# Constants and the roots' transposition under the keys' section, and earlier loads for mixing and the second gate

## The chip, the cores and the metric

The kernel runs on one core of one Trainium2 chip. The metric is the device time of one execution in microseconds (us). The engines are named as the profile names them: PE is TensorE, DVE is VectorE, ACT is ScalarE, POOL is GpSimd, and SP is SyncE, which here only issues transfers (DMA). All loads and stores of this kernel go through SP's one queue, in order.

## What is computed

One layer of a streaming encoder: an RMS norm, one projection of all rows into queries, keys, values and gates of two groups of eight heads, stick-breaking attention (group A) and forgetting attention (group B), each output times SiLU of its gate, an output projection, and a final norm. 2048 prompt rows with 16 meta rows in front, and 32 rows of a running stream with a cache of 2048 rows. The model width is 1024, a head has 64.

```python
def project(h, g_norm, w_in, b_f):
    u = rmsnorm(h, g_norm) @ w_in
    ...
    logf = jax.nn.log_sigmoid(fl.astype(jnp.float32) + b_f.astype(jnp.float32))

def sb_block(q, k, v, q_start):
    ...
    log_keep = jnp.where(before, jax.nn.log_sigmoid(-z), 0.0)
    later = lax.cumsum(log_keep, axis=3, reverse=True) - log_keep
    w = jnp.where(before, jnp.exp(jax.nn.log_sigmoid(z) + later), 0.0)

def fox_block(q, k, v, c, q_start):
    ...
    decay = c_q[:, :, :, None] - c_k[:, :, None, :]
    p = jax.nn.softmax(jnp.where(causal, logits + decay, -jnp.inf), axis=-1)

def combine(h, oa, ga, ob, gb, w_out):
    mixed = jnp.concatenate([oa.reshape(B, T, SB_WIDTH) * jax.nn.silu(ga),
                             ob.reshape(B, T, FOX_WIDTH) * jax.nn.silu(gb)], axis=-1)
    return h + mixed @ w_out
```

## The kernel before

All matrix products of the projections are made of three products of split operands: x and w are each cast to a high part and a low remainder, and `mm3` (line 288) adds hi x hi, hi x lo and lo x hi over eight slices of the width, 24 matmuls for one group of output.

**The values' section (v1).** `SecV.run` goes over 17 row tiles t of 128 rows, two units u of 256 columns each, so 34 groups of 24 matmuls (names psv). Beside it the generator `feed` brings the rows: for a tile it loads x_T (names xraw), casts it to xh on ACT (line 1562) and subtracts on DVE to xl; it also loads the same rows untransposed in two halves (xrow), sums their squares on ACT (line 1536), and at the tiles listed in ROOTS it computes the reciprocal roots r_all on DVE and ACT (`newton`, lines 600 to 606). A group of values needs its tile's root only when ACT evacuates it: vt is the PSUM result times r_all (line 430), fl the eight columns of the forget gate (line 432). The accumulators psv share four PSUM banks (pool ps_1), so group n + 4 waits for the evacuation of group n. The evacuated vt is stored twice (out_dram, v_s).

Staging tiles come from `stage(name, type, tag)`, two tiles to a tag. vt, and in later sections kf, have the tag "kt"; xrow, rrow and the prefix sums dc have the tag "sg". In the kernel before the constants' staging tiles mf, sf and one have the tag "kt" too, and `constants()` (line 167) is called in `feed` at tile 6: it loads masks, pick matrix, rows6 and biases b_bc, casts three of them on DVE, and writes rows of ones to kb_s (five writes).

At the end of `feed` the 17 columns of roots are transposed on PE (ptr, line 1576), copied by DVE (rrow) and written to r_s in DRAM. After the values, five reads bring them back spread over all partitions (xr), because the keys' evacuation multiplies by a row of roots.

**The keys' section (k1).** 384 columns of rows at a time, two units: PE makes psTk, DVE multiplies by xr to kf (line 400), ACT casts to kx (line 401), DVE subtracts, SP stores kx twice and kf once. It uses the same four banks. Beside it `decay` runs: it finishes the forget gates fl (lines 536 to 547: abs, exp, reciprocal, log), transposes them on PE (ptf_t, line 555, and ptf, line 589), and forms prefix sums (dcp, line 567).

**Later.** The query section q1, then the forgetting attention beside further projections, then from about 1060 us the stick-breaking attention (`sb_main`), beside which `filler` runs: the first gate's last part, the second gate g1 and the output projection of group B. For each group of g1 `ahead_g` loads the attention output (og) and the reciprocal denominators (den, two reads); POOL multiplies them (line 516), DVE multiplies by the gate (line 517), SP stores to m_s. All these tiles come from one tag "k2" of six tiles. `mixing(step)` starts a mix for each finished pair of A heads and block of 512 rows: `mix_a` loads oa and gfa, DVE multiplies (line 1339), ACT takes the sigmoid in place (line 1340), DVE multiplies again (line 1342), SP stores to m_s; MW = 2 steps of the attention lie between its parts.

**What sets the order.** The framework's scheduler places the instructions on each engine's queue by its own estimate of when they are ready; the order in the program counts as their rank. On the chip each queue then runs strictly in that order, so one instruction that waits holds all behind it.

Of the kernel before, what the change touches and what calls it, by code (L numbers as in the profile page):

```python
# [7 lines left out]
F32 = mybir.dt.float32  # L8
# [9 lines left out]
NS = 32  # L18
# [42 lines left out]
HB = 0.5  # L61
MW = 2
NL = 4.0
NA = 2.0
# [24 lines left out]
def trunk_step_kernel(ctx, tc, x_all, x_T, x_K, x_V, x_Q, ca_kT, ca_v, cb_kT, cb_v, cb_lfT, norm_g, w_K, b_f,  # L89
# [77 lines left out]
    def constants():  # L167
        mf = stage("mf", F32, "kt")[:, :SEC]
        dma(mf, mask_c)
        nc.vector.tensor_copy(masks16, mf)  # L170
        sf = stage("sf", F32, "kt")
        dma(sf[:, :2 * NS], smask_c)
        dma(sf[0:8, 2 * NS:2 * NS + 128], pick_c)
        dma(rows6[64:70], rows_c)
        nc.vector.tensor_copy(ident_r, ident)
        nc.vector.tensor_copy(smasks, sf[:, :2 * NS])
        nc.vector.tensor_copy(pick, sf[0:8, 2 * NS:2 * NS + 128])
        dma(b_bc, b_f[0:1, :].broadcast_to([128, 8]))
        dma(den_s[:, NX:TQ], ones_t[0:8, :NS])
        one = stage("one", F32, "kt")[0:8, :SEC]  # L180
        nc.gpsimd.memset(one, 1.0)
        for c in range(0, T, SEC):
            n = min(SEC, T - c)
            dma(kb_s[:, 130:134, c:c + n], one[:, :n].unsqueeze(1).broadcast_to([8, 4, n]))
# [126 lines left out]
    class SecT(Units):  # L311
# [9 lines left out]
        def unit(self, u):  # L321
            return load_unit(256, KT, f"{self.nm}{u}", g_col)

        def first_x(self):
            if self.xs is None:
                self.xs = self.src(self.nm, *self.chunks[0])

        def run(self):
# [11 lines left out]
            last = len(seq) - 1  # L340
            half = lead if lead == len(chunks) else last
            for c, (a, n, us) in enumerate(seq):
                xflush()
# [3 lines left out]
                elif self.next:  # L347
                    self.next.first_x()
                halves = ((a, n),) if n <= SEC else ((a, n // 2), (a + n // 2, n - n // 2))
                order = [(p, b, m) for u in us for b, m in halves for p in (2 * u, 2 * u + 1)]  # L350
                for i, (p, b, m) in enumerate(order):
# [4 lines left out]
                    if p == 2 and len(self.prep):  # L356
# [5 lines left out]
                                        [xh(k, b, m) for k in ks_], [xl(k, b, m) for k in ks_], m / 2.4), todo,  # L362
                                    self.ahead and (lambda p=p, b=b, m=m: self.ahead(p, b, m)), self.tick)

# [9 lines left out]
    def stage(nm, dt=F32, tag=None):  # L374
        return st_p.tile([128, SEC + 4], dt, tag=tag, name=nm)
# [129 lines left out]
    def evac_g(s):  # L505
        def f(ps, p, a, n, xr):
# [7 lines left out]
            nc.vector.tensor_tensor(sg, gf, sg, ALU.mult)  # L514
            o, rb = og.pop()
            nc.gpsimd.tensor_tensor(o, o, rb, ALU.mult)
# [986 lines left out]
    with ExitStack() as es:  # L1503
# [17 lines left out]
        def feed():  # L1521
# [27 lines left out]
            for t in range(NT):  # L1549
# [6 lines left out]
                if t == 0:  # L1556
                    yield 0.0
                if t == 6:
                    constants()
                raw = raw.rearrange("p (k c) -> p k c", k=KT)  # L1560
# [12 lines left out]
            squares(NT - 1)  # L1573
            root()
            pt = ps_t.tile([128, SEC], F32, tag="pt", name="ptr")
            nc.tensor.transpose(pt[:NT, :128], r_all, ident)
            row = stage("rrow", F32, "sg")[:NT, :128]
            nc.vector.tensor_copy(row, pt[:NT, :128])
            dma(r_s, row)
            yield 1.0  # L1580

# [42 lines left out]
        n_es.close()  # L1624
        for c, (a, n) in enumerate(CH_R):
            dma(xroot[c], r_row[:, a:a + n].broadcast_to([128, n]))
        mark("k1")
        d_es = ExitStack()
        dg = Pace(decay(d_es.enter_context(tc.tile_pool(name="d_p", bufs=1))))
        for i, c in enumerate(k1.run()):  # L1630
            if i % 4 == 3:
                dg.advance(1)
# [72 lines left out]
    def mixing(step):  # L1705
# [9 lines left out]
        if ready and mixed and len(mixes) < 2 and mixed[0][0] <= step:  # L1715
            _, p, g = mixed.pop(0)
            mixes.append([step + MW, g, mix_a(p, g * SEC, SEC if g < 4 else NS)])
            next(mixes[-1][2])
# [102 lines left out]
```

## Time and profile before

| | us |
|---|---|
| median of 3 runs | 1906.87 (1905.25 to 1909.02) |
| profiled execution, its own time | 1911.02 |
| its span, first to last instruction | 1909.3 |
| busy: PE, DVE, ACT, POOL | 1846.9, 1252.1, 1051.0, 1089.1 |
| mean granted clock of TensorE | 0.991 |

PE's busy share is 97%, so the question for any change is where the rest lies, and whether PE runs at 2.4 or 1.2 GHz (a granted clock of 1.00 or 0.50) while it is busy. The ends of matmuls are modelled, and a busy PE row overlaps its neighbour; the distance from start to start tells the pace.

### The profile page before, as it was taken

The page shows a single profiled execution, that of the slowest core. Times are in us where ns is not written, and L with a number is a line of the kernel's source. Part 1 is how long each engine was busy: PE and PEld are TensorE (multiplying, and loading weights), DVE is VectorE, ACT ScalarE, POOL GpSimd, SP SyncE. Part 2 cuts the span into 40 slices and gives each one's busy share as a digit, 9 for nine tenths or more (in the row PEclk, how much of TensorE's full clock was granted, in tenths as well). Part 3 has the DMA queues.
Part 4 walks back from the last instruction along what each step waited for, and adds up shares of the span by engine and source line. Part 5 has one row for each costly group of instructions (what it writes and reads, how often), then busy time and mean ns, then how long its engine had stood idle before and what let it go on. Part 6 is the DMA issues. An engine that isn't in the chain of part 4 may idle for free.

```text
span 1909.3 us, 35868 instructions
## 1 busy us (share of the span) xinstructions
PE 1846.9 (97%) x12096; PEld 1456.9 (76%) x12096; DVE 1252.1 (66%) x2342; ACT 1051.0 (55%) x2317; POOL 1089.1 (57%) x1643
## 2 busy tenths in 40 slices
PE   7999999999999999999999999999989999999998
PEld 6999998777767777777776788777767766676676
DVE  4236427656574455756655676788778988888776
ACT  5641213454455454644445667676757777777732
POOL 0000002787777687778877676667767766677400
PEclk8999999999999999999999999999999999999999
DMA  7865646566655344666677553654666454434455
GB/s 232 276 177 156 181 124 187 161 188 184 192 161 158 121 155 142 203 207 211 207 225 213 179 166 129 218 183 157 203 197 209 146 179 145 151 111 151 142 203 176
DMA packets 229438, 339.27 MB, mean 178 GB/s; under 512 B 46189, under 2 KB 154054, under 8 KB 220038
## 3 DMA queue, kind: packets, MB, share of 16 engines
q1 hardware_dynamic: 229254, 336.97, 57.0%
q8 instruction: 96, 1.57, 0.3%
q14 instruction: 88, 0.72, 0.1%
HBM read 220.20 MB, written 116.68 MB: 176 GB/s over the span
## 4 chain that ended last, share of the span: by engine, by line
PE 76%; DVE 8%; DMA 6%; ACT 4%; issue 3%; POOL 1%; SPq 1%; DVEq 0%; ACTq 0%; POOLq 0%
PE pob L731 7%; PE poa L731 5%; PE pta L870 4%; PE sb L1181 3%; PE psTk L292 3%; PE sb L1182 3%; PE smb L1153 3%; PE psv L292 3%; PE psTk L294 3%; PE psTk L293 3%; PE psTq L292 3%; PE psv L294 3%; PE psv L293 3%; PE psTq L293 3%; PE psTq L294 3%
## 5 line engine op out<-in xcount | busy, mean ns | idle before, releaser
L783 POOL TENSOR_TENSOR wa<-wa,mba 128x512 f32<-128x512 f32 (+1 forms) x320 | 366.1, 1147 | 141.4 <-DVE wa L777 127.8
L1195 POOL TENSOR_TENSOR accb<-accb,pfb 128x512 f32<-128x512 f32 (+1 forms) x256 | 297.9, 1163 | 97.9 <-ACT pfb L1185 76.9
L777 DVE TENSOR_TENSOR_SCAN wa<-sa,wa,ones_r 128x512 f32<-128x512 f32 x192 | 244.5, 1279 | 47.1 <-ACT sa L774 29.5
L1185 ACT ACTIVATE pfb<-sb 128x512 f32<-128x512 f32 (+1 forms) x320 | 175.8, 553 | 171.5 <-PE sb L1182 152.8
L1161 DVE TENSOR_REDUCE mxb<-smb 128x1 f32<-128x512 f32 (+1 forms) x320 | 195.2, 613 | 89.4 <-PE smb L1153 84.8
L873 ACT COPY ptha<-pta 128x512 f32<-128x512 f32 (+1 forms) x320 | 168.0, 527 | 86.1 <-PE pta L870 83.8
L870 PE MATMUL pta<-ident,wa 128*128 128x128 f32 x1088 | 175.9, 276 | 12.6 <-ACT ptha L873 3.8
L773 ACT ACTIVATE mba<-sa 128x512 f32<-128x512 f32 (+1 forms) x320 | 174.2, 545 | 20.1 <-POOL wa L783 17.2
L774 ACT ACTIVATE sa<-sa 128x512 f32<-128x512 f32 (+1 forms) x320 | 173.6, 543 | 0.0
L870 PEld LDWEIGHTS pta<-ident,wa 128*128 128x128 f32 x1088 | 127.8, 140 | 52.4 <-issue 21.1
L811 PE MATMUL sa<-kca,qaa 128*128 128x512 f32 (+3 forms) x352 | 150.7, 428 | 8.5 <-DVE wa L777 6.0
L292 PE MATMUL psTg<-xhg,whig 128*128 128x260 f32 x512 | 148.9, 291 | 0.0
L731 PE MATMUL pob<-pfb,vcb 128*64 128x512 f32 (+1 forms) x640 | 148.2, 563 | 0.0
L293 PE MATMUL psTg<-xlg,whig 128*128 128x260 f32 x512 | 145.1, 283 | 0.0
L294 PE MATMUL psTg<-xhg,wlog 128*128 128x260 f32 x512 | 145.0, 283 | 0.0
L731 PE MATMUL poa<-ptha,vca 128*64 128x512 f32 (+2 forms) x640 | 144.4, 562 | 0.0
L777 DVE TENSOR_TENSOR_SCAN wa<-sa,ones_r,m 128x512 f32<-128x512 f32 (+3 forms) x128 | 112.2, 880 | 34.8 <-ACT sa L774 25.2
L105 POOL MEMSET vm<- 128x128 f32 x2 | 0.3, 203 | 225.6 <-PE psTq L293 225.6
L1153 PE MATMUL smb<-k2b,q2b 66*128 66x512 f32 (+1 forms) x320 | 119.5, 373 | 4.9 <-DVE mxb L1161 4.1
L1181 PE MATMUL sb<-qab,kcb 128*128 128x512 f32 (+1 forms) x320 | 122.3, 382 | 1.3 <-ACT pfb L1185 1.3
L812 PE MATMUL sa<-kca,qz 128*128 128x512 f32 (+3 forms) x352 | 122.0, 359 | 0.0
L1182 PE MATMUL sb<-q2b,k2b 70*128 70x512 f32 (+1 forms) x320 | 119.4, 373 | 0.0
(280 smaller groups left out, 5231.1 us busy)
## 6 DMA issues: line engine op xcount, KB each, us to landing
xhg<-x_s SPq DMA_DIRECT2D x16, 1040.0 KB
xlg<-x_s SPq DMA_DIRECT2D x16, 1040.0 KB
xwk<-in_x_K_dram SPq DMA_DIRECT2D x8, 1048.0 KB
k_s<-kx SPq DMA_DIRECT2D x64, 131.0 KB
xwq<-in_x_Q_dram SPq DMA_DIRECT2D x8, 1040.0 KB
x_s<-xhq SPq DMA_DIRECT2D x8, 1040.0 KB
x_s<-xlq SPq DMA_DIRECT2D x8, 1040.0 KB
q_s<-q SPq DMA_DIRECT2D x64, 130.0 KB
```

The costliest lines, as they stand in the source:

```text
L292: nc.tensor.matmul(out, a_h[k], b_h[k], start=(k == 0), stop=False)
L293: nc.tensor.matmul(out, a_h[k], b_l[k], start=False, stop=False)
L294: nc.tensor.matmul(out, a_l[k], b_h[k], start=False, stop=(k == n - 1))
L731: nc.tensor.matmul(po[64 * side:64 * side + 64, :n], v, p[:, :n], start=first, stop=False)
L777: nc.vector.tensor_tensor_scan(out=w[:, 1:n + 1], data0=ps[:, :n], data1=m01[:, :n] if diag else ones_t[:, 0:1].broadcast_to([128, n]), in ...
L783: nc.gpsimd.tensor_tensor(w[:, :n], w[:, :n], take[:, :n], ALU.mult)
L870: nc.tensor.transpose(pt[:, b * 128:b * 128 + 128], self.w[b][:, c:c + 128], ident)
L1153: nc.tensor.matmul(ps[:, :SEC - s0 + m], q2[0:66, bs], k2[0:66, s0:SEC + m], start=True, stop=True)
L1161: nc.vector.tensor_reduce(mx[:, b, kc:kc + 1], ps[:, v0:v0 + nv + m], AX.X, ALU.max)
L1181: nc.tensor.matmul(ps[:, :n], hd.k[kc][:, js], self.qa[:, :n], start=True, stop=False)
L1182: nc.tensor.matmul(ps[:, :n], hd.k2[kc][:, js], self.q2[0:70, :n], start=False, stop=True)
L1195: nc.gpsimd.tensor_tensor(self.acc[:, :n], self.acc[:, :n], pf[:, :n], ALU.add)
```

## The change

Four things:

- `constants()` is no longer called in `feed`, but at the eleventh step of the keys (a step is three matmuls), and its staging tiles take the tag "sg".
- The transposition of the roots, its copy, the write to r_s and the five reads xr are a function `root_rows()`, called at the fifth step of the keys instead of the end of `feed`. `decay` advances from the twelfth step on.
- In g1 `ahead` loads for the group after the coming one (a list `coming`, whose first entry is loaded before the section), and `og` is taken from its front.
- A mix has ML = 5 steps between its loads and its first multiplication, instead of MW = 2.

```diff
...
 MW = 2
+ML = 5
 NL = 4.0
...
     def constants():
-        mf = stage("mf", F32, "kt")[:, :SEC]
+        mf = stage("mf", F32, "sg")[:, :SEC]
         dma(mf, mask_c)
         nc.vector.tensor_copy(masks16, mf)
-        sf = stage("sf", F32, "kt")
+        sf = stage("sf", F32, "sg")
         dma(sf[:, :2 * NS], smask_c)
...
         dma(den_s[:, NX:TQ], ones_t[0:8, :NS])
-        one = stage("one", F32, "kt")[0:8, :SEC]
+        one = stage("one", F32, "sg")[0:8, :SEC]
         nc.gpsimd.memset(one, 1.0)
...
 
+        def halves(self, a, n):
+            return ((a, n),) if n <= SEC else ((a, n // 2), (a + n // 2, n - n // 2))
+
         def first_x(self):
...
             half = lead if lead == len(chunks) else last
+            coming = [(p, b, m) for a, n, us in seq for u in us for b, m in self.halves(a, n)
+                      for p in (2 * u, 2 * u + 1)]
+            if self.ahead:
+                self.ahead(*coming.pop(0))
             for c, (a, n, us) in enumerate(seq):
...
                     self.next.first_x()
-                halves = ((a, n),) if n <= SEC else ((a, n // 2), (a + n // 2, n - n // 2))
-                order = [(p, b, m) for u in us for b, m in halves for p in (2 * u, 2 * u + 1)]
+                order = [(p, b, m) for u in us for b, m in self.halves(a, n) for p in (2 * u, 2 * u + 1)]
                 for i, (p, b, m) in enumerate(order):
...
                                         [xh(k, b, m) for k in ks_], [xl(k, b, m) for k in ks_], m / 2.4), todo,
-                                    self.ahead and (lambda p=p, b=b, m=m: self.ahead(p, b, m)), self.tick)
+                                    self.ahead and (lambda: coming and self.ahead(*coming.pop(0))), self.tick)
 
...
             nc.vector.tensor_tensor(sg, gf, sg, ALU.mult)
-            o, rb = og.pop()
+            o, rb = og.pop(0)
             nc.gpsimd.tensor_tensor(o, o, rb, ALU.mult)
...
                     yield 0.0
-                if t == 6:
-                    constants()
                 raw = raw.rearrange("p (k c) -> p k c", k=KT)
...
             root()
+            yield 1.0
+
+        def root_rows():
             pt = ps_t.tile([128, SEC], F32, tag="pt", name="ptr")
...
             dma(r_s, row)
-            yield 1.0
+            for c, (a, n) in enumerate(CH_R):
+                dma(xroot[c], r_row[:, a:a + n].broadcast_to([128, n]))
 
...
         n_es.close()
-        for c, (a, n) in enumerate(CH_R):
-            dma(xroot[c], r_row[:, a:a + n].broadcast_to([128, n]))
         mark("k1")
...
         for i, c in enumerate(k1.run()):
-            if i % 4 == 3:
+            if i == 4:
+                root_rows()
+            elif i == 10:
+                constants()
+            if i > 10 and i % 4 == 3:
                 dg.advance(1)
...
             _, p, g = mixed.pop(0)
-            mixes.append([step + MW, g, mix_a(p, g * SEC, SEC if g < 4 else NS)])
+            mixes.append([step + ML, g, mix_a(p, g * SEC, SEC if g < 4 else NS)])
             next(mixes[-1][2])
```

**Place 1, ACT in the values' section.** The stretch from the squares of tile 4 (xrow_0_298) on; vt_483 before and vt_464 after are the same evacuation, of psv_417. Before:

```order
L1536 ACTIVATE xrow_0_298,ss<-xrow_0_298 128x512
L1536 ACTIVATE xrow_1_299,ss<-xrow_1_299 128x512
L601 ACTIVATE r_all<-rs 128x2
L1536 ACTIVATE xrow_0_375,ss<-xrow_0_375 128x512
L1536 ACTIVATE xrow_1_376,ss<-xrow_1_376 128x512
L1562 CAST xh_166<-xraw_5_444 128x8x128
L430 ACTIVATE vt_483<-psv_417,r_all 128x256
L1536 ACTIVATE xrow_0_469,ss<-xrow_0_469 128x512
L430 ACTIVATE vt_512<-psv_476,r_all 128x256
```

After:

```order
L1543 ACTIVATE xrow_0_298,ss<-xrow_0_298 128x512
L1543 ACTIVATE xrow_1_299,ss<-xrow_1_299 128x512
L437 ACTIVATE vt_464<-psv_417,r_all 128x256
L608 ACTIVATE r_all<-rs 128x2
L437 ACTIVATE vt_493<-psv_457,r_all 128x256
L1543 ACTIVATE xrow_0_375,ss<-xrow_0_375 128x512
L1543 ACTIVATE xrow_1_376,ss<-xrow_1_376 128x512
L1567 CAST xh_166<-xraw_5_444 128x8x128
L1543 ACTIVATE xrow_0_450,ss<-xrow_0_450 128x512
L1543 ACTIVATE xrow_1_451,ss<-xrow_1_451 128x512
L437 ACTIVATE vt_532<-psv_486,r_all 128x256
L437 ACTIVATE vt_561<-psv_525,r_all 128x256
```

The evacuation of psv_417 stood behind the squares of tile 5 and the cast of tile 6 (xraw_5); now it stands behind the squares of tile 4, and the next one follows one row later.

**Place 2, PE, the transposition of the roots.** Before, among the values (psv_1241 is tile 13, first unit, with eight groups to come):

```order
L294 MATMUL psv_1241<-whiv_205,xl_155 128x264
L292 MATMUL psv_1241<-whiv_205,xh_154 128x264
L1576 MATMUL ptr<-ident,r_all 17x128
L293 MATMUL psv_1241<-wlov_206,xh_154 128x264
L294 MATMUL psv_1241<-whiv_205,xl_155 128x264
```

After, among the keys' first group (psTk_0_0), 15 matmuls in:

```order
L294 MATMUL psTk_0_0_1523<-xl_179,whik_1337 128x384
L295 MATMUL psTk_0_0_1523<-xh_178,wlok_1338 128x384
L1584 MATMUL ptr<-ident,r_all 17x128
L293 MATMUL psTk_0_0_1523<-xh_178,whik_1337 128x384
L294 MATMUL psTk_0_0_1523<-xl_179,whik_1337 128x384
```

The transposition of the forget gates, 48 matmuls into the keys before, now stands 86 matmuls in. No other row of PE moves.

**Place 3, DVE in the stick-breaking stage.** The mix of one block of rows, oa_1536, among the scans wa and the gate's multiplications (sg, og), near 1459 us. Before:

```order
L517 TENSOR_TENSOR og_1300_18303<-og_1300_18303,sg_1300_18445 128x260
L777 SCALAR_TENSOR_TENSOR wa_0_3_0_18431<-sa_0_3_0_18427,wa_0_2_0_18327,ones_r 128x512
L1339 TENSOR_TENSOR oa_1536_18372<-oa_1536_18372,gfa_1536_18373 128x512
L845 COPY p0a_0_17858<-wa_0_3_0_18431 128x1
L1342 TENSOR_TENSOR oa_1536_18372<-oa_1536_18372,gfa_1536_18373 128x512
L777 SCALAR_TENSOR_TENSOR wa_0_3_1_18476<-sa_0_3_1_18472,wa_0_2_1_18348,ones_r 128x512
L508 TENSOR_TENSOR gf_1300_18564<-psTg_1300_2_18400,xrg_1300_17697 128x260
```

After:

```order
L524 TENSOR_TENSOR og_1300_18199<-og_1300_18199,sg_1300_18447 128x260
L784 SCALAR_TENSOR_TENSOR wa_0_3_0_18434<-sa_0_3_0_18430,wa_0_2_0_18330,ones_r 128x512
L852 COPY p0a_0_17863<-wa_0_3_0_18434 128x1
L784 SCALAR_TENSOR_TENSOR wa_0_3_1_18478<-sa_0_3_1_18474,wa_0_2_1_18351,ones_r 128x512
L1346 TENSOR_TENSOR oa_1536_18376<-oa_1536_18376,gfa_1536_18377 128x512
L852 COPY p0a_0_17863<-wa_0_3_1_18478 128x1
L515 TENSOR_TENSOR gf_1300_18567<-psTg_1300_2_18403,xrg_1300_17700 128x260
```

The mix's first multiplication moved behind the next scan; its second (line 1342 before, 1349 after) moved six rows, out of the stretch shown. These are two of the 8 mixing multiplications, of 40, that moved at all.

## Rows read from the trace of the kernel before

**Rows 1.** The page: span and TensorE's busy time.

```profile
span 1909.3 us, 35868 instructions
...
PE 1846.9 (97%) x12096; PEld 1456.9 (76%) x12096; DVE 1252.1 (66%) x2342; ACT 1051.0 (55%) x2317; POOL 1089.1 (57%) x1643
```

**Rows 2.** Busy time by stage: stretch, its us, engines (instructions), PEclk, DMA share, GB/s.

```profile
0.00:130.30 130.30, 112.60 (x833) 106.52 (x834) 42.06 (x110) 69.45 (x169) 1.13 (x8) 0.93 0.76 241
130.30:176.20 45.90, 45.90 (x293) 45.05 (x292) 31.22 (x71) 12.08 (x24) 0.00 (x0) 1.00 0.53 135
...
1190.00:1660.00 470.00, 447.80 (x3055) 341.57 (x3055) 390.29 (x621) 337.17 (x754) 329.82 (x663) 0.99 0.57 180
```

**Rows 3.** TensorE's waits, 0 to 130.3 us: total us, times, longest.

```profile
PE psv L292 <- ACT vt L430: 6.8, 2, 6.1
PE ptr L1576 <- issue: 4.2, 1, 4.2
...
PE psv L292 <- ACT fl L432: 1.6, 1, 1.6
```

**Rows 4.** Chain of waits, 30 to 57 us: start us, us, what.

```profile
33.18 5.96 DMA mf<-in_mask_c_dram
...
41.28 0.48 ACT vt L430
...
48.30 6.43 DMA v_s<-vt
54.89 0.47 ACT vt L430
```

**Rows 5.** Timeline of SyncE's issues, 31 to 51 us: start us, us, transfer, how many.

```profile
32.64 0.43 SPq L99 DMA_DIRECT2D xraw<-in_x_T_dram  x1
...
40.30 3.97 SPq L99 DMA_DIRECT2D kb_s<-one  x5
...
46.62 0.43 SPq L99 DMA_DIRECT2D xraw<-in_x_T_dram  x1
```

**Rows 6.** Busy time in three stretches of the values' section.

```profile
41.81:47.30 5.49, 5.49 (x24) 5.19 (x24) 0.00 (x0) 0.56 (x2) 0.00 (x0) 0.50 0.52 83
...
70.00:100.00 30.00, 30.00 (x253) 30.00 (x252) 10.02 (x22) 19.19 (x46) 0.00 (x0) 1.00 0.91 298
104.64:109.07 4.43, 4.43 (x25) 4.43 (x26) 0.29 (x2) 0.64 (x2) 0.00 (x0) 0.62 0.52 177
```

**Rows 7.** Timeline of SyncE, x_T loads of tiles 9 and 15.

```profile
59.77 0.66 SPq L99 DMA_DIRECT2D xraw<-in_x_T_dram  x1
...
92.08 0.52 SPq L99 DMA_DIRECT2D xraw<-in_x_T_dram  x1
```

**Rows 8.** Timeline of SyncE: a write to DRAM and the read that waits for it, twice.

```profile
105.23 0.24 SPq L99 DMA_DIRECT2D r_s<-rrow  x1
...
108.09 1.36 SPq L99 DMA_DIRECT2D xr<-r_s  x3
...
1071.16 0.32 SPq L99 DMA_DIRECT2D rd_s<-den  x1
1072.84 1.12 SPq L99 DMA_DIRECT2D den<-rd_s  x2
```

**Rows 9.** Timeline of the keys' section: ScalarE, VectorE, TensorE.

```profile
131.34 0.31 ACT L537 ACTIVATE fe<-fl 128x136 f32<-128x136 f32 x1
...
136.52 0.56 DVE L400 TENSOR_TENSOR kf<-psTk,xr 128x384 f32<-128x384 f32 x1
137.00 0.29 DVE L547 TENSOR_TENSOR fl<-fl,fe 128x136 f32<-128x136 f32 x1
...
138.80 0.20 PE L555 MATMUL ptf_t<-ident,fl 48*8 48x48 f32 x1
```

**Rows 10.** Waits of VectorE and GpSimd, 1190 to 1660 us: total us, times, longest.

```profile
DVE oa L1339 <- DMA gfa<-gf_s: 18.4, 9, 4.3
...
POOL og L516 <- DMA den<-rd_s: 15.7, 13, 3.7
```

## The prediction

> **What bounds the kernel now.** I read the page first. TensorE is busy for 1846.9 of 1909.3 us [rows 1], so whatever this change gains can only come out of the 62.4 us in which TensorE stands still, and out of the stretches in which its granted clock is the lower of its two levels. The busy times by stage [rows 2] say where these are: the values' section (0 to 130.3 us) has 17.7 us of idle time and a mean granted clock of 0.93; the keys' section behind it has none at all; the stage from 1190 to 1660 us, where the stick-breaking heads run beside the second gate and the mixing, has 22.2 us. The change touches all three.
>
> In the values' section the list of TensorE's waits [rows 3] names three that matter: one of 6.1 us (and a second, 0.7 us) for ScalarE's evacuation vt, one of 4.2 us at ptr, which is the transposition of the roots, and one of 1.6 us for fl. The chain of waits explains the first [rows 4]: the masks' load mf takes 5.96 us from its issue, VectorE casts it, and only then does ScalarE write vt at 41.28 us. The code says why they hang together: mf, sf and one take staging tiles of tag "kt", of which there are two, and vt needs one. The SyncE queue has the other half [rows 5]: the x_T load of tile 6 is issued at 32.64 us, that of tile 7 at 46.62 us, with the five writes of ones and their wait in between. Hence the two later entries of the chain, a v_s write that lands after 6.43 us and an evacuation at 54.89 us, behind which the 1.6 us wait stands.
>
> TensorE's clock adds to this. After the long wait 24 matmuls took 5.49 us at a granted clock of 0.50, which is 1.2 GHz; the undisturbed stretch from 70 to 100 us has 253 in 30.00 us at 1.00, so 0.1186 us each and 2.85 us for 24 [rows 6]. That is 2.6 us lost. Behind ptr 25 matmuls took 4.43 us instead of 25 x 0.1186 = 2.97: 1.5 us more.
>
> **The change part by part.** (1) *Constants out of the values' section.* In the order of the changed kernel vt of the next two groups stands right behind the squares of tile 4, before anything that a constant holds. So the 6.1, 0.7 and 1.6 us go, and the 2.6 us at half clock: 11.0 us. What is late next: ScalarE's evacuations still stand in line with the squares of the rows and the casts of x_T. Walking the new order with the durations of the rows, the tile 6 cast, the squares and the next two evacuations end near 41 us, when TensorE would want their banks at 41.3; if a v_s write takes 6.43 us again, as in [rows 4], it is 43.5. Later groups come out at nearly nothing to spare. Bounds: 0 and 4 us for the whole section. I take 1.7, near the lower end, because from 70 to 100 us nothing waits at a DMA share of 0.91 [rows 6], and because the x_T loads of tiles 9 and 15 are issued 32.31 us apart [rows 7], 5.39 us a tile, while TensorE needs 48 x 0.1186 = 5.69.
>
> (2) *Transposition of the roots under the keys.* In front of ptr TensorE waits for the last root, and it has eight more groups of the values that need none. The 4.2 us and the 1.5 us at half clock go: 5.7 us. The transposition itself is kept. In its new place, 15 matmuls into the keys, its roots have long been ready.
>
> (3) *What the keys' section gets.* Let T0 be its start. The first key evacuation needs xr, so now ptr, its copy, the write r_s and the read xr stand ahead of it. Four PSUM banks cover that: the fifth group starts at 4 x 24 x 0.177 = 17 us (48 matmuls took from 130.30 to 138.80 us [rows 9]). The narrower place is another. The forget gates' transposition ptf_t now stands behind 86 matmuls, at T0 + 15.3 us, and it waits for the finished fl, whose VectorE operations stand in line behind the first key evacuation. I price that line: ptr, copy and the queue's turn, 3.5 us; r_s from write to readable, 1.7 us by the rd_s pair and at most 2.9 by the r_s pair [rows 8], say 2.3; two issues, 0.9; the landing of xr, for which no row stands alone, between 1.7 and the 5.96 of mf, say 3.0, since DMA is far less loaded here (0.53 against 0.76 [rows 2]). The first kf then starts at T0 + 9.7. From there to the finished fl: evacuation, cast, and the steps that took from 131.34 to 137.29 us in the trace [rows 9], less 0.9 of other work among them, so 1.5 + 5.1 = 6.6 to 7.0 us. That ends at T0 + 16.3 to 16.7, and TensorE waits 1.0 to 1.4 us, with the pick's load on top 1.5. With every landing at its short end it is 0; with both at 5.96 us it is 7.8 and half clock behind. I take 1.5. The ones' writes stand in SyncE ahead of later key exports, and VectorE's second prefix sum waits for them; by the same rows that is over at T0 + 24, and the bank behind it is wanted at T0 + 31. That costs nothing as long as the banks cover it. The small constants cost TensorE nothing: masks, pick and biases are first used long behind.
>
> The Trainium skill (DMA: Bandwidth & Descriptors, section "Anatomy of one DMA") gives a DMA a fixed cost of about 2.0 us, most of it the receipt of the write, fitted for transfers issued by GpSimd. By it both hops of the roots would be 2.0 us, TensorE would wait about 0.4 us, and the total would be 1.1 us lower.
>
> (4) *Loads for mixing and second gate in advance.* The waits are there: VectorE waits 18.4 us for gfa, GpSimd 15.7 us for den [rows 10]. But the order of the changed kernel hardly moves: of 32 gate multiplications on GpSimd 26 stand in the same row, of 40 mixing operations on VectorE 32, and the loads on SyncE stand where they stood, but for one mix and a few groups near the end of the gate. The scheduler had already put them as early as free tiles allow; each of the six tiles of tag "k2" comes free when it did. So I cost this at nothing, with -2 to +2 us for the few rows that move. The three extra steps of a mix could hold the last chunks' loads, but TensorE's order there is the same row by row.
>
> **The sum.** -11.0 - 5.7 + 1.7 + 1.5 + 0 = -13.5 us. The profiled execution took 1911.02 us (1909.3 of it the span), the median of the runs is 1906.87. The same program was 4 us apart there, so I take the difference to the median: 1906.87 - 13.5 = 1893.4 us.
>
> **The rivals.** *The loads set the pace.* Without the pause the values' section has no slack left, and evacuations behind late rows hold TensorE several times. For it: a DMA share of 0.91 and the 6.43 us landing. Against it: 5.39 us a tile. It gives back 0.3 us in each of nine tiles and one stretch at half clock (2.6), so 5 to 6 us: 1899. *The keys wait for the roots.* Both landings take what mf took: TensorE waits 7.8 us at ptf_t, and half clock costs 1.5 behind it, 9.3 in place of 1.5: 1901. Against it: mf flew in a jam. *The loads in advance do work.* Of the 22.2 us idle in the stage [rows 2] the waits behind a VectorE or ScalarE held by gfa go, at most some 8 us: 1885. Against it: the rows that did not move. *Slower than before.* The same place at ptf_t, but each of the two hops takes over some 11 us, because the ones' writes, the weights and the key exports share the queue; then the wait eats the 15 us gained ahead of it and the 3.8 us up to a measurable loss. With 12 us a hop the wait is 19.9 us, and with 1.5 behind it the total about 1913. No row shows a landing above 6.43 us.
>
> **How the numbers follow.** Forecast 0.69 (1889 to 1897); loads set the pace 0.14 (1899); keys wait for the roots 0.08 (1901); loads in advance work 0.06 (1885); slower 0.03. Forecast and first rival hold 0.83, so the range is 1888.5 to 1899.5. What this kernel's runs can tell from no change is about 0.2%, 3.8 us: below 1903.1 counts as faster. That is nearly every case but the last, less a little for a bad key section: faster 0.94, same 0.03, slower 0.03.
>
> **What would show it.** In the changed profile: no wait for vt above 2.5 us and no stretch at clock 0.50 between 35 and 115 us; the values end near 115 us instead of 130.3; ptr without idle time in front of it; a wait of 0 to 3 us in front of ptf_t; the attention begins some 13 us earlier, and from there to the end both kernels take the same within 3 us. I am wrong if the values' section still waits for rows or v_s writes in many places, if ptf_t costs more than 4 us, or if the stage with the second gate changes by more than 5 us either way.

## The result and the profile after

The changed kernel takes 1895.4 us (median of 5 runs, 1890.85 to 1898.28), against 1906.87 us for the kernel before, now with 5 runs (1901.05 to 1909.02). The ratio is 0.994, with a 95% interval of 0.9922 to 0.9957, so 11.4 us less (8.2 to 14.9). On another chip the same pair gave 0.9927 (0.9909 to 0.9945), 14.0 us less. The forecast was 13.5 us less, 1893.4 us.

The profiled execution took 1892.88 us. Its page begins with the span and the busy times:

```profile
span 1891.2 us, 35859 instructions
...
PE 1840.1 (97%) x12096; PEld 1451.4 (77%) x12096; DVE 1246.3 (66%) x2342; ACT 1050.8 (56%) x2317; POOL 1088.4 (58%) x1643
```

The busy time of TensorE fell by 6.8 us against [rows 1], though it runs the same matmuls: fewer of them ran at half clock. The rest of the 18.1 us of span is idle time. Busy time by stage in the changed kernel (stretch, its us, engines, granted clock, DMA share, GB/s): the values' section, the first 45.90 us of the keys, the keys, the stage with the second gate:

```profile
0.00:115.24 115.24, 107.24 (x832) 102.27 (x833) 41.05 (x105) 69.67 (x169) 0.61 (x7) 0.97 0.81 258
115.24:161.14 45.90, 44.90 (x284) 43.91 (x283) 28.53 (x67) 11.21 (x22) 0.51 (x1) 1.00 0.56 147
115.24:210.10 94.86, 93.86 (x596) 92.87 (x595) 53.80 (x117) 21.73 (x45) 0.51 (x1) 1.00 0.63 171
...
1047.40:1518.43 471.03, 453.85 (x3300) 362.89 (x3301) 375.28 (x612) 336.19 (x752) 340.11 (x696) 1.00 0.57 178
```

The first line stands against the first of [rows 2]. The section is 15.1 us shorter, its idle time fell from 17.7 to 8.0 us, and its clock rose from 0.93 to 0.97. The keys had no idle time and have 1.00 us now. TensorE's waits from 30 to 240 us (total us, times, longest) say which one that is:

```profile
PE psv L293 <- ACT vt L437: 1.1, 1, 1.1
PE ptf_t L562 <- DVE fl L554: 1.0, 1, 1.0
PE psv L293 <- ACT fl L439: 0.2, 1, 0.2
```

These three answer to [rows 3]: 12.6 us before, 2.3 us after, and ptr no longer among them. The timeline of ScalarE shows what place 1 of the order said: the two evacuations that came at 41.28 us [rows 4] and later now stand directly behind the squares of tile 4.

```profile
33.30 0.47 ACT L437 ACTIVATE vt<-psv,r_all 128x256 f32<-128x256 f32 x1
...
33.99 0.47 ACT L437 ACTIVATE vt<-psv,r_all 128x256 f32<-128x256 f32 x1
```

After the long wait of the kernel before 24 matmuls ran at 0.50, from 41.81 to 47.30 us [rows 6]; now the granted clock is 1.00 from 41.54 to 47.00 us:

```profile
41.54:47.00 5.46, 4.35 (x37) 4.13 (x36) 0.00 (x0) 2.69 (x7) 0.00 (x0) 1.00 0.94 286
```

### The profile page after: what moved, and what is told of

Its sections match the earlier page's. It is cut to its first block, busy times and chain, and to the rows that moved or that the text cites. A ratio compares the mean times of both kernels' runs of the same rounds, so it can differ in the third digit from the quotient of the medians.

```text
span 1891.2 us, 35859 instructions
## 1 busy us (share of the span) xinstructions
PE 1840.1 (97%) x12096; PEld 1451.4 (77%) x12096; DVE 1246.3 (66%) x2342; ACT 1050.8 (56%) x2317; POOL 1088.4 (58%) x1643
## 4 chain that ended last, share of the span: by engine, by line
PE 74%; DVE 8%; DMA 7%; ACT 4%; issue 3%; POOL 2%; SPq 1%; DVEq 0%; ACTq 0%; POOLq 0%
PE pob L738 7%; PE poa L738 5%; PE pta L877 5%; PE sb L1188 3%; PE sb L1189 3%; PE smb L1160 3%; PE psTk L293 3%; PE psTq L293 3%; PE psTk L295 3%; PE psTk L294 3%; PE psTq L294 3%; PE psTq L295 3%; PE sa L819 3%; PE sa L818 3%; PE psTg L293 2%
## 5 line engine op out<-in xcount | busy, mean ns | idle before, releaser
L780 ACT ACTIVATE mba<-sa 128x512 f32<-128x512 f32 (+1 forms) x320 | 174.6, 546 | 20.1 <-POOL wa L790 15.3
L293 PEld LDWEIGHTS psTg<-xhg,whig 128*128 128x128 f32 x512 | 96.5, 189 | 9.8 <-issue 2.8
```

The lines of the kernel that those rows point to most:

```text
L293: nc.tensor.matmul(out, a_h[k], b_h[k], start=(k == 0), stop=False)
```

## Experiments

Each is compared with runs of the kernel before on the same chip; a difference in us is the ratio applied to their median, with the 95% interval. A profile is one execution of each.

### The constants alone, the roots alone

```diff
...
-                if t == 6:
-                    constants()
...
+            if i == 10:
+                constants()
+            if i > 10 and i % 4 == 3:
```

> Only the constants move under the keys (with the staging tag sg, and decay from the twelfth step on); the roots are transposed at the end of the values as before. If the terms of the forecast are right: the values' section loses the waits for vt and fl and the half clock behind them, 11.0 us, and gets up to 1.7 us of new waits, so the keys start near 121 us instead of 130.3; the 4.2 us in front of ptr and the 1.5 us at half clock stay; ptf_t waits under 1 us, because xr is on its way before the keys begin. Total about -9 us against the kernel before. If the loads set the pace instead: several waits for rows or v_s writes between 35 and 115 us, and -3 to -5 us.

Measured: 0.9951 (0.9935 to 0.9967), 9.4 us less (6.3 to 12.4). The keys began at 118.03 us. In this kernel's order the constants do not stand under the keys: SyncE issues the masks' load at 91.98 us and the first write of ones at 104.09 us, still among the values but behind the last rows. Only one wait is left from 30 to 240 us:

```profile
PE ptr L1574 <- issue: 1.9, 1, 1.9
```

No wait for rows, stores or evacuations took the place of the removed ones, so the loads do not set the pace. The wait at ptr did not stay at 4.2 us but fell to 1.9. Why is open: rows, and with them roots, that are no longer held back at tile 7 would fit, but it falls to 1.6 us as well in a kernel further down (the constants in tiles of their own) in which the rows are still held back.

```diff
...
-            dma(r_s, row)
-            yield 1.0
...
+            if i == 4:
+                root_rows()
```

> Only the transposition of the roots, r_s and the reads xr move to the fifth step of the keys; constants and loads as before. By the forecast ptr loses its 4.2 us wait and the 1.5 us at half clock: the keys start near 124.6 us; the fl steps stand ahead of the first kf in VectorE's order here, so ptf_t does not wait for xr; total -5.7 us. If the late xr holds the keys through their banks instead: a wait for kf of some us in the first 20 us of the keys, and -2 us or less.

Measured: 0.9969 (0.9954 to 0.9984), 5.9 us less (3.1 to 8.8). The one wait left from 30 to 240 us is that for vt, and the keys are as long as before:

```profile
PE psv L292 <- ACT vt L430: 6.6, 2, 5.9
```

Both parts do what they were priced at. Apart they give 9.4 + 5.9 = 15.3 us, together (below) 11.8: the intervals allow plain addition, but the profiles show an overlap too, 2.3 us at ptr that the constants alone already take away.

### The loads in advance, alone and left out

```diff
...
-            mixes.append([step + MW, g, mix_a(p, g * SEC, SEC if g < 4 else NS)])
+            mixes.append([step + ML, g, mix_a(p, g * SEC, SEC if g < 4 else NS)])
...
+            if self.ahead:
+                self.ahead(*coming.pop(0))
...
-            o, rb = og.pop()
+            o, rb = og.pop(0)
```

> Only the loads in advance (ML = 5 and the loads of the second gate one group earlier). By the forecast 0 us (within 2), and the stage from the first query of the second group of heads to the output projection as long as before. If the loads do work: -4 us, the amount by which the stage with the second gate and the mixing was shorter in the profile of the changed kernel than in that of before.

> The loads in advance alone, once more. Up to the second gate its queues are those of the kernel before row by row, yet its forgetting attention took 699.0 us against 695.4. By the theory of differences between executions that stage comes out elsewhere this time (694 to 700), and the median is within 0.2% of the kernel before. If the loads in advance gain in the last two stages of the stick-breaking attention (473.8 and 267.3 against 475.0 and 269.8): the last of them is below 268 us again.

Measured: 1.0017 (1.0002 to 1.0032) the first time, 3.2 us more, and 0.9995 (0.9982 to 1.0009) the second, 1.0 us less. The two together show no difference. Left out of the changed kernel:

> The changed kernel without its loads in advance: constants and roots under the keys, ML = MW = 2 and the old place of the second gate's loads. By the forecast the same as the changed kernel, -11.5 to -13.5 us against the kernel before. If the loads in advance brought the 4 us that the second gate's stage was shorter: -7.5 to -9.5 us.

Measured: 0.9938 (0.9918 to 0.9957), 11.8 us less (8.2 to 15.7), as the changed kernel (11.4 and 14.0). So the loads bring nothing to the total that these runs can tell.

Why, then, was the second gate's stage 4.0 us shorter in the first profile of the changed kernel (471.03 against 474.99 us)? The changed kernel was profiled once more:

> The changed kernel once more, for a second profiled execution and more runs of the time. By the theory that its later stages differ from those of the kernel before only from execution to execution: the forgetting attention (before 695.4 us, first profile of the changed kernel 697.5) and the stage of the second gate (475.0 and 471.0) come out anywhere between these, and the median is 11 to 13 us below the kernel before. If the changed loads are behind these differences: 697 to 698 and 471 again.

Its median was 1899.59 us, with the ratio of 0.9927 told above, and the stage took 476.09 us:

```profile
1045.99:1522.08 476.09, 455.66 (x3300) 364.37 (x3301) 377.67 (x612) 336.41 (x752) 339.51 (x696) 0.99 0.57 176
```

One program gives 471.03 and 476.09, which is more than the difference to be explained. The forgetting attention shows it more plainly. Up to the second gate the kernel with the loads alone has the queues of the kernel before, row by row. In that kernel before, in it, and in its repetition, each in a fence of its own, the stage took 695.35, 698.97 and 698.07 us:

```profile
324.45:1019.80 695.35, 686.90 (x4617) 512.11 (x4616) 420.48 (x855) 344.84 (x736) 533.80 (x538) 1.00 0.58 179
```

```profile
324.32:1023.29 698.97, 689.61 (x4618) 513.23 (x4617) 420.13 (x855) 344.34 (x736) 533.28 (x538) 1.00 0.59 178
```

```profile
321.53:1019.60 698.07, 688.74 (x4617) 513.02 (x4616) 420.60 (x855) 344.27 (x736) 533.08 (x538) 1.00 0.59 178
```

A difference of 3 to 4 us in a long stage of a single profile is therefore no evidence.

The waits themselves are better evidence, for they come back in every execution. One wait of 1.1 to 1.5 us, some 226 us into the last stage of the stick-breaking attention (the one that begins with the output projection), stands in every profile with the old loads (before, each of the two parts alone, both without the loads, and the three kernels of the next section) and in none with ML = 5. In the kernel before GpSimd, VectorE, ScalarE and TensorE show it, in this order of cause:

```profile
1757.09 1.64 POOL L783 TENSOR_TENSOR wa<-wa,mba 128x512 f32<-128x512 f32 x1 [0.46 <-DVE wa L777]
```

```profile
1757.57 1.71 DVE L1339 TENSOR_TENSOR oa<-oa,gfa 128x512 f32<-128x512 f32 x1
```

```profile
1759.31 0.63 ACT L1340 ACTIVATE gfa<-gfa 128x512 f32<-128x512 f32 x1 [2.18 <-DVE oa L1339]
```

```profile
1760.56 0.63 PE L870 MATMUL pta<-ident,wa 128*128 128x128 f32 x4 [1.50 <-ACT ptha L873]
```

The sigmoid of the mix sits on ScalarE ahead of the copies ptha that TensorE needs, and waits for the mix's multiplication. The loads of that mix are not late, for VectorE does not stand idle ahead of it. The multiplication itself takes 1.71 us instead of 0.66: it starts inside a product wa of GpSimd and ends 0.55 us behind it. In the changed kernel another operation of VectorE stands at this place and takes 1.72 us, and the mix comes behind the product:

```profile
1740.94 1.72 DVE L103 TENSOR_TENSOR mxl<-mxw,mxh 128x512 fp32r<-128x512 f32 x1
...
1742.85 0.66 DVE L1346 TENSOR_TENSOR oa<-oa,gfa 128x512 f32<-128x512 f32 x1
```

So ML = 5 helps here by the place of the mix, and not by an earlier load. It shows in the length of this last stage too. In five of the seven profiles with ML = 5 the stage takes 267.3 to 267.8 us, among them the repetition of the loads alone (267.77 us, where the expectation asked for less than 268); in the seven with the old loads it takes 268.3 to 271.2. The other two with ML = 5, the last two kernels below, have 269.2 and 268.7. By the means, 267.9 and 269.7, the gain is some 1.8 us, less than the totals can tell.

In its place a new wait has come 260 us into the gate's stage, in every profile with both changed loads. In the changed kernel, GpSimd and then TensorE:

```profile
1305.27 0.86 POOL L523 TENSOR_TENSOR og<-og,den 128x260 f32<-128x260 f32 x1 [1.27 <-DMA den<-rd_s]
```

```profile
1307.58 0.33 PE L877 MATMUL pta<-ident,wa 128*128 128x128 f32 x1 [1.19 <-POOL wa L790]
```

Here the gate's product, placed earlier on GpSimd, waits for its own load and holds the product wa of the attention behind it. One wait of this size is gone, one has come.

### What in the constants costs

The prediction put the 6.1 us down to the staging tiles and named SyncE's queue beside them. Three kernels, all from the kernel before with the constants left at tile 6, take these apart. First, staging tiles of their own:

```diff
...
-        mf = stage("mf", F32, "kt")[:, :SEC]
+        mf = cst("mf", SEC)[:, :SEC]
...
-        one = stage("one", F32, "kt")[0:8, :SEC]
+        one = cst("mf", SEC)[0:8, :SEC]
```

> The kernel before, constants still at tile 6, but mf, sf and one get staging tiles of their own (not those of vt); only the small load of pick with its cast moves to the keys. The loads and the five writes of ones stand in SyncE's queue as before. If the shared staging tiles alone hold ScalarE: the waits for vt (6.8 us) and the half clock behind them (2.6 us) go, the values end near 121 us, total -8 to -9 us. If the queue does it too (the stores of vt, which free its tiles, and the x_T load stand behind the ones, and these wait for the masks' load): a wait for vt of 3 us or more stays, with half clock behind it, and the total is -4 us or less.

Measured: 0.9995 (0.9982 to 1.0008), 1.0 us less (3.4 less to 1.5 more). The evacuations come early, as in the changed kernel, but ScalarE is then caught one tile later (timeline; in brackets the idle time before and what ended it):

```profile
32.88 0.47 ACT L428 ACTIVATE vt<-psv,r_all 128x256 f32<-128x256 f32 x1
...
33.67 0.48 ACT L428 ACTIVATE vt<-psv,r_all 128x256 f32<-128x256 f32 x1
...
47.26 0.63 ACT L1534 ACTIVATE xrow<-xrow 128x512 f32<-128x512 f32 x1 [7.47 <-DMA xrow<-in_x_all_dram]
```

and TensorE with it:

```profile
48.50 0.58 PE L290 MATMUL psv<-whiv,xh 128*128 128x256 f32 x1 [6.72 <-ACT vt L428]
```

SyncE shows why. The ones reuse the masks' tile, so their writes wait until the masks have landed and been cast, and the rows stand behind them:

```profile
39.33 3.92 SPq L99 DMA_DIRECT2D kb_s<-mf  x5
43.35 1.18 SPq L99 DMA_DIRECT2D xrow<-in_x_all_dram  x1
```

The long wait kept its length, 6.72 us for 6.14 us [rows 3], with the rows' load at its end instead of the masks'. The second expectation holds. In this one profile the keys still began 6.9 us earlier than before, at 123.39 us, since the waits at fl and ptr shrank and part of the half clock fell into the wait. The twelve runs do not bear that out as a gain; what differs between the executions is open.

Second, the tile of ones alone made its own, so that SyncE no longer stands still for the masks while the five writes stay:

```diff
...
-        one = stage("one", F32, "kt")[0:8, :SEC]
+        one = cst("one", SEC)[0:8, :SEC]
```

> The kernel before, constants at tile 6, masks and pick staged in the tiles of vt as before; only the tile of ones is one of its own, filled without waiting for the masks. So the five writes of ones stay in SyncE's queue (3.9 us of issues and their traffic), but no longer hold the queue until the masks have landed and been cast. If that hold is what costs (seen with the ones moved away: 8 us less; with staging tiles of their own and the hold kept: nothing measurable): the writes are issued from 36 us instead of 40, the x_T load of tile 7 before 43 us instead of 46.6, and the total is -4 to -8 us. If the writes themselves cost, by their issues and traffic: the long wait stays above 5 us and the total is -2 us or less.

Measured: 0.9972 (0.9961 to 0.9984), 5.3 us less (3.1 to 7.4). The writes go out from 37.30 us, 3.0 us earlier than in [rows 5], though the masks' load stood 1.2 us later in this execution. The x_T load of tile 7 came at 46.07 us, only 0.55 us earlier than before, and not before 43 as expected. The row of the five writes spans 4.90 us because SyncE waits 2.0 us behind the first of them until the x_T load of tile 6 has landed:

```profile
37.30 4.90 SPq L99 DMA_DIRECT2D kb_s<-one  x5
...
46.07 0.39 SPq L99 DMA_DIRECT2D xraw<-in_x_T_dram  x1
```

TensorE's waits for vt fall to 4.0 us in two; it came 2.8 us later to the first of these places than in the kernel before, so some of the fall is only shifted:

```profile
PE psv L292 <- ACT vt L430: 4.0, 2, 2.9
...
PE ptr L1576 <- issue: 1.8, 1, 1.8
```

The keys began at 123.42 us, no earlier than with all staging tiles apart, so the two profiles do not tell these kernels from each other; the runs do (5.3 us against 1.0), with intervals that just touch. Nor does this kernel test the queue by itself: with a tile of its own the ones also no longer take one of the two tiles of vt.

Third, only the ones (memset and writes) moved under the keys; masks, pick and biases stay at tile 6 in the tiles of vt:

```diff
...
+            if i == 10:
+                ones_rows()
```

> The kernel before, with only the memset of one and the five writes of ones moved to the eleventh step of the keys; masks, pick, rows6 and biases load at tile 6 into the tiles of vt as before. If the staging tiles hold ScalarE by the masks' load alone: the wait for vt stays, 4 to 6 us with half clock behind it, because mf still needs its 6 us, and only what came behind it goes (0.7 and 1.6 us, and some of the 4.2 us at ptr, as tile 7 loads earlier): -2 to -5 us. If the ones are the main cost: the wait for vt falls below 2 us and the total is -8 us or more.

Measured: 0.9957 (0.9942 to 0.9971), 8.2 us less (5.5 to 11.1). ScalarE now waits for the masks' and the pick's casts, but for 0.18 and 1.05 us:

```profile
39.06 0.47 ACT L432 ACTIVATE vt<-psv,r_all 128x256 f32<-128x256 f32 x1 [0.18 <-DVE masks L170]
40.58 0.47 ACT L432 ACTIVATE vt<-psv,r_all 128x256 f32<-128x256 f32 x1 [1.05 <-DVE pick L177]
```

TensorE waited 1.6 us there; it came 2.3 us later to that bank than in the kernel before, after a wait of 3.9 us at 21 us, so some of the gain at this place is only shifted. The time decides: 8.2 us less, of 9.4 for all constants. So the ones were most of the cost. How it divides is not shown. The steps from 1.0 to 5.3, 8.2 and 9.4 us are differences of measurements that carry some 2 to 3 us each, and each kernel that changes the ones frees a tile of vt along with the queue. What agrees with their order are TensorE's waits from 30 us to the end of the values: 12.6 us before, then 8.3 with all staging tiles apart, 5.8 with the ones in a tile of their own, 3.4 with the ones moved and 1.9 with all constants moved.

### The keys' new wait

The prediction's chain for the wait at ptf_t runs through xr, the first kf and fl. One kernel lengthens it by three copies from DRAM to DRAM, one shortens it by calling `root_rows()` at the first step:

```diff
...
-            dma(r_s, row)
+            dma(hop[0], row)
+            dma(hop[1], hop[0])
+            dma(hop[2], hop[1])
+            dma(r_s, hop[2])
```

> The changed kernel with three more copies from DRAM to DRAM between the write of the roots and the reads xr, so that xr comes later by three round trips of 1.7 to 2.9 us each (5 to 9 us). Theory of the prediction (ptf_t waits for fl, fl for the first kf, kf for xr): the 1.0 us in front of ptf_t grows by as much, to 6 to 10 us, with half clock behind it (1.5 us), and the total is 6 to 11 us above the changed kernel, that is 2 to 6 us below the kernel before. If the chain does not run through xr: ptf_t waits 1 us and the total is that of the changed kernel.

> The changed kernel with the roots' transposition at the first step of the keys instead of the fifth: 12 matmuls, some 2.1 us, earlier. Theory of the chain through xr: the wait at ptf_t (1.0 us) falls to 0, the keys take 93.7 us instead of 94.9, and the total is 1 us below the changed kernel, less than these runs can tell. If the transposition then waits for the last root: a wait of up to 2 us in front of ptr.

Measured: with the copies 0.9942 (0.9925 to 0.9959), 11.1 us less than before, where the changed kernel beside it had 14.0 less; at the first step 0.9928 (0.9909 to 0.9946), 13.8 us less. The wait grew to 1.95 us only, not to 6 to 10, and the reason shows in the queues: with the longer chain the scheduler put ptf_t behind 118 matmuls of the keys instead of 86, 32 x 0.177 = 5.7 us later. SyncE, VectorE and TensorE of the kernel with the copies:

```profile
119.70 0.22 SPq L100 DMA_DIRECT2D hop<-rrow  x1
...
122.62 0.57 SPq L100 DMA_DIRECT2D hop<-hop  x1
...
125.36 0.48 SPq L100 DMA_DIRECT2D hop<-hop  x1
...
127.25 0.47 SPq L100 DMA_DIRECT2D r_s<-hop  x1
...
129.36 2.24 SPq L100 DMA_DIRECT2D xr<-r_s  x5
```

```profile
132.60 1.02 DVE L408 TENSOR_TENSOR kf<-psTk,xr 128x384 f32<-128x384 f32 x2 [5.36 <-issue]
```

```profile
139.32 0.20 PE L563 MATMUL ptf_t<-ident,fl 48*8 48x48 f32 x1 [1.95 <-DVE fl L555]
```

Its keys begin at 116.02 us, so the first kf starts 16.6 us into them. In the changed kernel (keys from 115.24 us) it is 10.1:

```profile
125.38 1.02 DVE L407 TENSOR_TENSOR kf<-psTk,xr 128x384 f32<-128x384 f32 x2 [1.09 <-issue]
...
131.19 0.30 DVE L554 TENSOR_TENSOR fl<-fl,fe 128x136 f32<-128x136 f32 x1
```

So kf came 6.4 us later and ptf_t 5.7 us later: 1.0 + 6.4 - 5.7 = 1.7 us, against the 1.95 measured. With the roots first kf came 8.8 us into the keys and the wait was 0.43 us; in the second profile of the changed kernel kf came after 11.4 us and the wait was 2.31. The wait follows kf each time, so the chain stands, while the size of the experiment with the copies missed.

The queues show one more link. In the changed kernel the read xr stands in SyncE's queue behind the load sf of the small masks, and sf is issued only when the masks' load has landed and been cast, for it reuses a staging tile. VectorE and SyncE:

```profile
120.89 0.43 DVE L171 CAST masks<-mf 128x512 bf16<-128x512 f32 x1 [2.37 <-DMA mf<-in_mask_c_dram]
```

```profile
121.34 0.35 SPq L100 DMA_DIRECT2D sf<-in_smask_c_dram  x1
```

With the roots first sf stands behind xr, and the read is issued 1.87 us after the write, instead of 2.99 us in the changed kernel:

```profile
118.36 0.28 SPq L100 DMA_DIRECT2D r_s<-rrow  x1
...
120.23 2.22 SPq L100 DMA_DIRECT2D xr<-r_s  x5
```

So of the 1.4 us by which kf came earlier into the keys there 1.1 are due to this order, and the write of the roots came only 0.6 us earlier; the reads took 0.3 us longer. The scheduler also put ptf_t behind 82 matmuls instead of 86, so a wait of 0.43 us was left where none was expected.

Last, a kernel for a better time: roots first, the forget gates' chain from the 24th step, the second gate's loads in their old place, ML = 5 kept.

```diff
...
-            if i == 4:
+            if i == 0:
...
-            if i > 10 and i % 4 == 3:
+            if i > 22 and i % 4 == 3:
```

> The changed kernel with three differences: the roots' transposition at the first step of the keys, the forget gates' chain from the 24th step on (its transposition ptf_t then stands behind 108 matmuls of the keys, 19 us, instead of 86), and the second gate's loads in their old place, with ML = 5 kept. Theory of the chain through xr: no wait at ptf_t, keys in 93.7 us instead of 94.9 to 96.2. The wait of 1.3 us that all kernels with both changed loads show 260 us into the second gate's stage goes if the gate's earlier loads cause it; the wait of 1.1 to 1.5 us 226 us into the last stage, which all kernels with the old loads show, stays away if ML = 5 removed it. Then the total is 2 to 4 us below the changed kernel. If neither: within 1 us of it.

Measured: 0.9948 (0.993 to 0.9966), 9.9 us less than before. No wait at ptf_t (ptf_t stood 108 matmuls in), the wait 260 us into the gate's stage gone, the one of the last stage still gone. The three waits went as expected, but the total missed the expectation, for it is no better than that of the changed kernel: each of these waits is 1 to 2 us long, and executions differ by more.

## Why the prediction was right, point by point

**The values' section.** It was to end near 115 us; it ended at 115.24, 113.78 and 115.12 us in the changed kernel, its second profile, and the kernel without the loads. Of the bounds of 0 to 4 us for what is late next 1.7 was taken. In the changed kernel 1.1 and 0.2 us were measured, the first before 42.93 us at the bank that was walked to 41.3; in its second profile nothing, without the loads 2.2 us and with the copies 2.4. So the bounds held, and that the single figure lay near is in part luck. The rival in which the loads set the pace falls with this.

**Its cause.** Here the prediction was right in the sum and weak in the split. It led with the masks' load and the shared staging tiles and gave the queue "the other half". With the tiles taken away alone a wait of 6.72 us stayed and the runs gained nothing measurable; with the ones alone moved they gained 8.2 us. What fell short is the reading of the chain in [rows 4] as the explanation: it names the event that came last, and behind it stood a second one (the rows held on SyncE) of the same length, ready to take its place. The change moved both, so the sum held. How much belongs to the queue and how much to the tile of vt that the ones occupy is open.

**The roots.** Priced at 5.7 us, measured alone 5.9. What the prediction did not see is that part of the wait at ptr was the constants' doing: with them gone alone it was 1.9 us instead of 4.2. So its first two terms share some 2 us, too little to show in totals that lie 8.2 to 14.9 us below.

**The keys.** First kf at 10.1 and 11.4 us (9.7 predicted), fl finished after 16.2 us (16.3 to 16.7), ptf_t waits 1.0 and 2.3 us (1.0 to 1.4, 1.5 with the pick), the keys longer by 1.2 and 2.5 us. The terms under it are less good than their sum. From the write r_s at 118.79 us to the issue of xr at 121.78 us 2.99 us passed (2.3 plus an issue was taken), but this is not the time until r_s can be read, which is at most 1.87 us: the rest is the queue, held by sf as shown above. The prediction had put the small constants at nothing there. From the issue of xr to kf 3.6 and 5.3 us passed (3.0 taken). What made up for part of it, by luck, is the way from kf to the finished fl, 6.1 us in both profiles (6.6 to 7.0 taken).

```profile
118.79 0.25 SPq L100 DMA_DIRECT2D r_s<-rrow  x1
...
121.78 2.28 SPq L100 DMA_DIRECT2D xr<-r_s  x5
```

The Trainium skill (DMA: Bandwidth & Descriptors, section "Anatomy of one DMA") gives about 2.0 us as the fixed cost of a transfer issued by GpSimd; with it for each hop, an estimate, the prediction's terms add up to a wait of 0.2 us and 1.3 us less in total (it wrote 0.4 and 1.1). The first hop agrees where nothing holds the queue, at 1.87 us; the second, five reads of 192 to 280 KB, does not, at 3.6 and 5.3 us to the first use.

**The loads in advance.** Costed at 0 with 2 us to either side; measured 3.2 more, 1.0 less, and no difference when left out. The reason given, that the order hardly moves, was the right one for the total. Of the few rows that move one takes away a wait of 1.1 to 1.5 us and one brings a wait of 1.2 to 1.7.

**The rest.** From the first query's attention to the end 1584.9 us before, 1580.6 and 1583.8 after. The first lies 4.3 us off, beyond the 3 us that the prediction allowed; the second profile of the same kernel does not, and the differences between executions of one program cover it. The same holds for 18.1 us between the two profiled spans and 11.4 between the medians: the step from one profile to the median was made by the medians, which was the safer one.

## What to carry to other kernels

A load or store that waits at the head of an in-order DMA queue costs everything behind it; look for what a queue's waiting instruction waits for before counting its bytes, and move or unchain that one first (here five small writes, made to wait by a reused tile, and what stood behind them were 8.2 of 9.4 us). The changed kernel made the same mistake once more under the keys, on a smaller scale: a load that waits for a staging tile stood ahead of the read that mattered. Where two mechanisms hold the same place, the trace names the later one, and removing it alone may gain little. Before explaining a few microseconds in a long stage, look at a second execution, and compare waits that come back rather than lengths.

## What the runs showed of the hardware

- Stages of 470 to 700 us with identical queues differ by 1 to 5 us from one execution to the next (695.35, 698.07 and 698.97 us; 471.03 and 476.09 us).
- A small transfer from DRAM to DRAM and the next that waits for it lie 1.9 to 2.7 us apart, in a stretch with other traffic (122.62 to 125.36 to 127.25 to 129.36 us); a small write from SBUF and the read that waits for it, with two other issues between them, 1.87 us (118.36 to 120.23 us).
- The five writes of broadcast ones occupy SyncE's queue for 3.92 us (constants in tiles of their own) to 4.48 us (roots first) by their issues alone; 4.90 us with a wait of 2.0 us among them.
- A multiplication of two 128 x 512 tiles on VectorE (the mix) that starts inside a product of two tiles on GpSimd, with 0.2 us or more of it still to run, ends 0.54 to 0.55 us behind that product. In the profile of the kernel before this holds in all twelve such cases, which take 0.77 to 1.77 us; the others take 0.66 to 0.69 us. At 1757.57 us TensorE paid for it with the 1.50 us shown above.
